# A two-layer encoder trunk on one core: weights of the up and down products laid out with two or four tiles of columns interleaved

## The chip, the cores and the metric

The kernel runs on one core of a Trainium2 chip. The metric is the device time of one execution in microseconds; lower is better. TensorE (PE) multiplies: it first loads a stationary operand of up to 128 x 128 (the instruction LDWEIGHTS, in the profile on a row of its own, PEld) and then streams a moving operand of up to 512 columns past it (MATMUL). VectorE (DVE), ScalarE (ACT) and GpSimd (POOL) do the rest; SyncE (SP) issues most transfers.

## What is computed

The reference takes x (512 tokens of width 1024) through two layers, in float32:

```
for i in range(DEPTH):                                   # DEPTH = 2
    h = rms_norm(x, attn_norm[i])
    mix = diff_attention(...) if i == 0 else gla_attention(...)
    cross = memory_cross_attention(...)
    x = x + concatenate([mix, cross]) @ w_out[i]
    h = rms_norm(x, ffn_norm[i])
    x = x + conv_ffn(h, w_up[i], conv_w[i], conv_b[i], w_down[i])

def conv_ffn(h, w_up, conv_w, conv_b, w_down):
    u = h @ w_up                       # 1024 -> 2 * 2816
    c = causal depthwise conv of width 3 over tokens (u) + conv_b
    a, g = split(c, 2)
    return (silu(g) * a) @ w_down      # 2816 -> 1024
```

The change lies in the two products of conv_ffn.

## The kernel before, in words

Activations lie transposed, features on the 128 partitions and the 512 tokens along the free dimension. For accuracy each float32 operand is split into a high part (rounded to the reduced float32 that TensorE takes at one pass) and a low part, and each product is made of three matmuls: high x high, high x low, low x high.

Weights come from one packed array, wpack, which the host lays out block by block in the order of use (function kernel, L1346 to L1351). A block is 128 partitions x 1024 floats. load_raw (L235) brings a block into a tile raw by a transfer on SP's queue, split_weights (L226) makes whi on ScalarE (the cast, L227) and wlo on VectorE (the difference, L230). _pieces (L57) lists the pieces of weights in order, _blocks (L95) cuts them into blocks, make_piece (L271) loads and splits them, prefetch (L289) keeps up to five blocks ahead.

Two groups of products use these weights as the stationary operand:

- The up products. w_up has 2 x 22 tiles of 128 columns (tile i of the half that becomes a, and of the half that is gated). One piece ("u", layer, i, half) is a block of eight tiles, one for each of the eight k of the contraction, tile k at columns 128 k to 128 k + 127. product (L343) takes hi[:, blk(n)] and lo[:, blk(n)] of each part as stationary operand and streams 512 tokens (L348 to L350): 24 matmuls for each piece.
- The down products. The 22 tiles of the middle are taken in three groups of 3, 4 and 4 pairs (GROUPS, L31). For each group the function down (L1154) forms seven products of sums of half blocks (a scheme in the manner of Strassen, with names such as a11, s1, a12) for each of two halves of the output: 14 steps. The sums are made of whole raw tiles by sum_weights (L242), and make_sum (L257) splits them (L263, L265). A step runs over the pairs k and, for each, two tiles n of 128 output features: stationary hi[:, 256 k + 128 n : ... + 128] or lo of the same, moving 256 tokens, both moving operand and output taken in reversed order (L1173). That makes 3 x 2 x 3 = 18 matmuls a step in the first group and 24 in the other two.

_ffn (L47) sets the order: up tiles 0 to 6, down group 0, up tiles 7 to 14, down group 1, up tiles 15 to 21, down group 2. TensorE's order is written out by hand; the up stages let VectorE and ScalarE work on convolution and SiLU, the down stages on adding each step's output into x (add, L1176) and on the weights of the steps to come.

In between, other projections (gemm, L314) use the weights as the moving operand; they are not touched.

Of the kernel before, what the change touches and what calls it, by code (L numbers as in the profile page):

```python
# [41 lines left out]
PASS = ([[(c, (0, 1, 2)) for c in C4], [(c, (3, 6, 7, 4, 5)) for c in C4]],  # L42
        [[(c, (0, 1, 2, 6, 7)) for c in (0, 1, 2)] + [(3, (0, 1, 2))],
         [(c, (3, 4, 5)) for c in (0, 1, 2)] + [(3, (6, 7, 3, 4, 5))]])


def _ffn():  # L47
# [9 lines left out]
def _pieces():  # L57

    plan = []

    def piece(key, name, i, ks, *ranges):
        plan.append((key, name, i, ks, ranges))

    for l in range(2):
        if l == 0:
            w = "w_in_diff"
            piece(("qk", 0), w, 0, K8, (0, 256), (768, 1024))
            piece(("vm", 0), w, 0, K8, (1536, 1792), (2304, 2560))
            piece(("qk", 1), w, 0, K8, (256, 512), (1024, 1280))
            piece(("kv", 0), "w_mem_kv", 0, K8, (0, 512))  # L70
            piece(("v", 1), w, 0, K8, (1792, 2304))
            piece(("qk", 2), w, 0, K8, (512, 768), (1280, 1536))
            piece(("kv", 1), "w_mem_kv", 1, K8, (0, 512))
        else:
            w = "w_in_gla"
            for i, ks in enumerate((GM[:3], GM[3:])):
                piece(("gm", i), w, 0, ks, (2304, 2576))
            for c in range(5):
                piece(("g", c), w, 0, K8, (512 * c, min(512 * c + 512, 2304)))
        for i, part in enumerate(PASS[l]):  # L80
            for c, ks in part:
                piece(("o", l, i, c), "w_out", l, ks, (256 * c, 256 * c + 256))
        base = 0
        for what, i in _ffn():
            if what == "up":
                for h in range(2):
                    f = DFF * h + 128 * i
                    piece(("u", l, i, h), "w_up", l, K8, (f, f + 128))
            else:
                for c, name in DOWN:  # L90
                    piece(("d", l, i, c, name), "w_down", l, (), (512 * c, 512 * c + 512))
    return plan


def _blocks():  # L95

    out = []
    for key, name, i, ks, ranges in _pieces():
        w = sum(b - a for a, b in ranges)
        if key[0] == "d":  # L100
            base, (f, _) = sum(GROUPS[:key[2]]), ranges[0]
            ks = [tuple(2 * q + j for q in range(base, base + GROUPS[key[2]])) for j in range(2)]
            out.append([(name, i, ks[j], ((f + 256 * h, f + 256 * h + 256),), 256)
                        for h, j in ((0, 0), (1, 0), (1, 1), (0, 1))] if key[4] == "a11" else [])
            continue
        step = WTILE // w
        out.append([(name, i, ks[j:j + step], ranges, w) for j in range(0, len(ks), step)])
    return out


# [40 lines left out]
def trunk(ctx, tc, head_d, x_t, mem_t, wpack, cols_a_d, cols_d, conv_d, gate_d, rel_bias, diff_lambda, consts, onehot, out):  # L151
# [31 lines left out]
    def blk(b, w=128):  # L183
        return slice(w * b, w * b + w)
# [36 lines left out]


    plan, blocks, made = _pieces(), _blocks(), []
    at = [0]

    def split_weights(c, raw, hi, lo, pin=False):  # L226
        ins = A.copy(hi[:, c], raw[:, c])  # L227
        if pin:
            tc.keep_in_program_order(ins)
        V.tensor_sub(lo[:, c], raw[:, c], hi[:, c].bitcast(F32))  # L230

    def raw_tile():
        return wp.tile([128, WTILE], F32, name="raw", tag="raw", bufs=RAWS)

    def load_raw(raw, n):  # L235
        nc.sync.dma_start(raw[:, :n], wpack[at[0], :, :n])
        at[0] += 1
        return raw
# [32 lines left out]
    def make_piece(raws=None, between=None):  # L271
        key = plan[len(made)][0]
        if key[0] == "d":
            made.append(make_sum(key))
            return
        parts = []
        for i, (_, _, kk, _, w) in enumerate(blocks[len(made)]):
            n = len(kk)
            raw = load_raw(raw_tile(), n * w) if raws is None else raws[i]
            hi, lo = (wp.tile([128, WTILE], F32R, name=t, tag=t, bufs=WB) for t in ("whi", "wlo"))  # L280
            if between is not None and i == 3:
                between()
            split_weights(slice(0, n * w), raw, hi, lo, len(made) == 2)
            parts += [(hi[:, blk(j, w)], lo[:, blk(j, w)]) for j in range(n)]
        made.append(parts)

    used = [0]
# [147 lines left out]
    with tc.tile_pool(name="ini", bufs=1) as ip, tc.manual_schedule(engines={E.Activation, E.DVE, E.Pool, E.SP}):  # L435
# [7 lines left out]
        p = bank("tp")  # L443
# [24 lines left out]
        parts, acc, split_w = [], [None], [None]  # L468
# [20 lines left out]
        for k in range(KT):  # L489
# [12 lines left out]
            hi, lo = parts[k]  # L502
            terms = (xh[k], hi), (xh[k], lo), (xl[k], hi)
            todo = [(b, i) for b in range(NB) for i in range(3)]
            for b, i in sorted(todo, key=lambda bi: bi[1]) if k == 0 else todo:
                xp, w = terms[i]
# [599 lines left out]
    def ffn(pool, l, acc):  # L1106
# [47 lines left out]
        def down(g, mids, finish):  # L1154
            last, ks = len(mids) - 1, tuple(range(len(mids)))
            parts, banks, first, last_group = {}, {}, used[0], g + 1 == len(GROUPS)

            def step(c, tag, w, m, ks=ks, start=False, more=True):
                if (c, w) not in parts:
                    parts[c, w] = weights(("d", l, g, c, w), more)  # L1160
                elif more:
                    prefetch(first + more)
                if start:
                    banks[c, tag] = bank(tag)
                p = banks[c, tag]
                hi, lo = parts[c, w]
                for k in ks:
                    mh, ml = mids[k][m]
                    for n in range(2):
                        o, ws = p[:, blk(n, 256)], slice(256 * k + 128 * n, 256 * k + 128 * n + 128)  # L1170
                        terms = (hi, mh), (hi, ml), (lo, mh)
                        for i, (a, b) in enumerate(terms):
                            mm(o[:, ::-1], a[:, ws], b[:, ::-1], start=start and (k, n, i) == (0, 0, 0), stop=k == last and i == 2,  # L1173
                               skip_group_check=True)

            def add(c, tag, f, t):  # L1176
                x = xpair[2 * c + f][:, :, blk(t, 256)]
                V.tensor_add(x, x, banks[c, tag].rearrange("p (n s) -> p n s", n=2))  # L1178

            def done(c, f, t=None):  # L1180
                for n in range(2):
                    finish(4 * c + 2 * f + n, t)
            if not last_group:
                step(0, "lg", "a11", "b11", start=True)
                add(0, "lg", 0, 0)
                step(0, "tp", "s1", "t1", start=True)
                add(0, "tp", 1, 1)
                step(0, "mm", "a12", "b21", start=True)
                add(0, "mm", 0, 0)
            else:  # L1190
                step(0, "lg", "a11", "b11", ks[:-1], True)
                step(0, "tp", "s1", "t1", ks[:-1], True, False)
                step(0, "mm", "a12", "b21", ks[:-1], True, False)
                step(0, "lg", "a11", "b11", ks[-1:], more=False)
                add(0, "lg", 0, 0)
                step(0, "tp", "s1", "t1", ks[-1:], more=1)
                add(0, "tp", 1, 1)
                step(0, "mm", "a12", "b21", ks[-1:], more=2)
                add(0, "mm", 0, 0)
            step(0, "lg", "s2", "t2")  # L1200
            add(0, "lg", 0, 1)
            step(0, "tp", "s4", "b22")
            add(0, "tp", 0, 1)
            step(0, "lg", "s3", "t3")
            add(0, "lg", 1, 1)
            step(1, "lg", "a11", "b11", start=True)
            add(1, "lg", 0, 0)
            step(0, "lg", "a22", "t4")
            add(0, "lg", 1, 0)
            done(0, 0)  # L1210
            step(1, "tp", "s1", "t1", start=True)
            add(1, "tp", 1, 1)
            step(1, "lg", "s2", "t2")
            add(1, "lg", 0, 1)
            done(0, 1)
            if l == 0 and last_group:
                tables("natural_log_exp_and_others")
            step(1, "mm", "a12", "b21", start=True)
            add(1, "mm", 0, 0)
            done(1, 0, 0)  # L1220
            step(1, "lg", "s3", "t3")
            add(1, "lg", 1, 1)
            done(1, 1, 1)
            step(1, "tp", "s4", "b22")
            add(1, "tp", 0, 1)
            done(1, 0, 1)
            step(1, "lg", "a22", "t4")
            add(1, "lg", 1, 0)
            done(1, 1, 0)
# [38 lines left out]
        for what, i in _ffn():  # L1268
            if what == "up":
# [12 lines left out]
                if i % 2 == 0:  # L1282
                    w = pool.tile([128, 8, 256], F32, name="w", bufs=1)
# [3 lines left out]
            else:  # L1287
                n, last = GROUPS[i], i == len(GROUPS) - 1
# [93 lines left out]
```

## Time and profile before

| what | us |
|---|---|
| median of the runs shown (2 runs, 1168.51 to 1169.13) | 1168.82 |
| the profiled execution, its own time | 1169.78 |
| its span, from the first to the last instruction | 1167.9 |
| third up stage of layer 0 (up tiles 15 to 21), stretch 490.1 to 566.2 | 76.1 |
| second down group of layer 0, stretch 450.3 to 490.1 | 39.8 |
| third down group of layer 0, stretch 566.2 to 607.8 | 41.6 |

Columns of a profile's views: a timeline row is start in us, length in us, engine, line of the kernel, operation, tiles (out<-in), partitions x elements, count. In the chain of work that ended last, a row is start, length, what. A group row has count, busy us, mean ns of one, and the idle time before. Matmuls overlap each other in the records, since one is still draining while the next streams: the pace is the distance from one start to the next, not the length of one. The same holds for the loads.

### The profile page before, as it was taken

How to read it: one execution, taken by the hardware profiler on the slowest of the kernel's cores; microseconds unless marked ns; L12 is line 12 of the kernel's file. 1: busy time of each engine (PE TensorE's matmuls, PEld its weight loads, DVE VectorE, ACT ScalarE, POOL GpSimd, SP SyncE). 2: the span in 40 equal slices, each digit the busy share in tenths (PEclk: the TensorE clock that was granted, in tenths of full speed). 3: DMA queues.
4: the chain of work that ended last, by engine and by line, in shares of the span. 5: the costliest groups of instructions: out<-in, count | busy, mean ns of one | idle time of the engine just before them, and what ended most of it. 6: DMA issues, size and time to landing. Idle time of an engine off the chain costs nothing.

```text
span 1167.9 us, 16705 instructions
## 1 busy us (share of the span) xinstructions
PE 1153.8 (99%) x6448; PEld 986.4 (84%) x6448; DVE 886.4 (76%) x1454; ACT 598.9 (51%) x1048; POOL 4.1 (0%) x17
## 2 busy tenths in 40 slices
PE   9999999999999999999999999999999999999998
PEld 6877777788899889988898788988789988998888
DVE  7746677679986778668897746868998777876885
ACT  6847677556443444344467534436654344434441
POOL 0000000000000000000000000000000000000000
PEclk9999999999999999999999999999999999999999
DMA  8533213233126322522253221144222532253212
GB/s 289 176 99 99 68 55 125 61 112 105 63 67 195 91 73 72 163 91 72 66 157 124 73 73 46 47 161 126 86 68 64 183 105 74 73 150 103 72 37 73
DMA packets 39853, 117.94 MB, mean 101 GB/s; under 512 B 4735, under 2 KB 7608, under 8 KB 39774
## 3 DMA queue, kind: packets, MB, share of 16 engines
q1 hardware_dynamic: 39630, 116.62, 32.1%
q8 instruction: 51, 0.84, 0.3%
q10 hardware_dynamic: 144, 0.26, 0.1%
q14 instruction: 28, 0.23, 0.1%
HBM read 112.65 MB, written 4.21 MB: 100 GB/s over the span
## 4 chain that ended last, share of the span: by engine, by line
PE 86%; DVE 8%; ACT 2%; DMA 1%; issue 1%; SPq 0%; DVEq 0%; ACTq 0%
PE ps_mm L348 9%; PE ps_mm L349 9%; PE ps_mm L350 9%; PE ps_lg L1173 8%; PE ps_sm L348 7%; PE ps_sm L350 7%; PE ps_sm L349 7%; PE ps_mm L327 5%; PE ps_mm L329 5%; PE ps_mm L328 5%; PE ps_tp L1173 4%; PE ps_mm L1173 2%; PE ps_tp L196 2%; DVE wlo L265 1%; PE ps_lg L686 1%; PE ps_sm L722 1%
## 5 line engine op out<-in xcount | busy, mean ns | idle before, releaser
L230 DVE TENSOR_TENSOR wlo<-raw,whi 128x1024 fp32r<-128x1024 f32 (+4 forms) x164 | 186.5, 1140 | 86.4 <-ACT whi L227 85.4
L227 ACT CAST whi<-raw 128x1024 fp32r<-128x1024 f32 (+4 forms) x164 | 160.7, 986 | 154.2 <-PE ps_sm L349 69.7
L348 PE MATMUL ps_mm<-x,whi 128*128 128x512 f32 x438 | 172.6, 394 | 0.3 <-DVE midh L1264 0.3
L349 PE MATMUL ps_mm<-x,whi 128*128 128x512 f32 x438 | 170.6, 389 | 0.2 <-DVE x L309 0.2
L350 PE MATMUL ps_mm<-x,wlo 128*128 128x512 f32 x438 | 170.6, 390 | 0.0
L348 PE MATMUL ps_sm<-x,whi 128*128 128x512 f32 x378 | 148.0, 391 | 0.0
L350 PE MATMUL ps_sm<-x,wlo 128*128 128x512 f32 x378 | 147.1, 389 | 0.0
L349 PE MATMUL ps_sm<-x,whi 128*128 128x512 f32 x378 | 147.1, 389 | 0.0
L327 PE MATMUL ps_mm<-whi,x 128*128 128x512 f32 (+2 forms) x336 | 132.0, 393 | 0.0
L329 PE MATMUL ps_mm<-whi,x 128*128 128x512 f32 (+2 forms) x336 | 126.7, 377 | 0.5 <-DVE x L309 0.4
L328 PE MATMUL ps_mm<-wlo,x 128*128 128x512 f32 (+2 forms) x336 | 126.0, 375 | 0.0
L263 ACT CAST whi<-raw 128x1024 fp32r<-128x1024 f32 (+1 forms) x60 | 58.4, 979 | 85.6 <-PE ps_sm L349 26.2
L348 PEld LDWEIGHTS ps_mm<-x,whi 128*128 128x128 f32 x438 | 82.3, 188 | 17.3 <-issue 0.9
L350 PEld LDWEIGHTS ps_mm<-x,wlo 128*128 128x128 f32 x438 | 82.2, 188 | 17.3
L349 PEld LDWEIGHTS ps_mm<-x,whi 128*128 128x128 f32 x438 | 82.3, 188 | 16.9 <-DVE x L309 0.6
L265 DVE TENSOR_TENSOR wlo<-raw,whi 128x1024 fp32r<-128x1024 f32 (+1 forms) x60 | 67.9, 1131 | 24.8 <-ACT whi L263 24.8
L349 PEld LDWEIGHTS ps_sm<-x,whi 128*128 128x128 f32 x378 | 71.0, 188 | 14.9 <-issue 0.5
L348 PEld LDWEIGHTS ps_sm<-x,whi 128*128 128x128 f32 x378 | 71.0, 188 | 14.9 <-issue 0.5
L350 PEld LDWEIGHTS ps_sm<-x,wlo 128*128 128x128 f32 x378 | 71.0, 188 | 14.9
L1173 PE MATMUL ps_lg<-midh,whi 128*128 128x256 f32 x264 | 74.8, 283 | 2.4 <-DVE x L1178 2.4
L1173 PE MATMUL ps_lg<-midh,wlo 128*128 128x256 f32 x264 | 74.3, 282 | 0.0
L1173 PE MATMUL ps_lg<-midl,whi 128*128 128x256 f32 x264 | 74.3, 282 | 0.0
(308 smaller groups left out, 2279.6 us busy)
## 6 DMA issues: line engine op xcount, KB each, us to landing
raw<-in_wpack_dram SPq DMA_DIRECT2D x170, 512.0 KB, 3.6
raw<-in_wpack_dram SPq DMA_DIRECT2D x24, 384.0 KB, 3.1
x<-in_x_t_dram SPq DMA_DIRECT2D x15, 256.0 KB, 5.4
xres<-x SPq DMA_DIRECT2D x8, 256.0 KB, 3.7
x<-xres SPq DMA_DIRECT2D x8, 256.0 KB, 4.6
raw<-in_wpack_dram SPq DMA_DIRECT2D x7, 256.0 KB, 6.7
bt<-bias_d SPq DMA_DIRECT2D x6, 256.0 KB, 5.1
x<-in_mem_t_dram SPq DMA_DIRECT2D x4, 256.0 KB, 6.0
```

Source lines behind the costliest of these rows:

```text
L196: nc.tensor.transpose(dst, src, ident[:n, :n])
L227: ins = A.copy(hi[:, c], raw[:, c])
L230: V.tensor_sub(lo[:, c], raw[:, c], hi[:, c].bitcast(F32))
L263: A.copy(hi[:, c], raw[:, c])
L265: todo = [lambda: V.tensor_sub(lo[:, c], raw[:, c], hi[:, c].bitcast(F32)), lambda: [sum_weights((*key[:3], *x)) for x in after]]
L327: mm(p, sh[k][:, blk(b)], hi, start=k == 0, stop=False)
L328: mm(p, sh[k][:, blk(b)], lo, start=False, stop=False)
L329: mm(p, sl[k][:, blk(b)], hi, start=False, stop=k == KT - 1)
L348: mm(p, hi[:, blk(n)], bh, start=i == first, stop=False)
L349: mm(p, hi[:, blk(n)], bl, start=False, stop=False)
L350: mm(p, lo[:, blk(n)], bh, start=False, stop=i == last)
L1173: mm(o[:, ::-1], a[:, ws], b[:, ::-1], start=start and (k, n, i) == (0, 0, 0), stop=k == last and i == 2, skip_group_check=True)
```

## The change

Within a block, tiles of 128 columns are interleaved in twos or fours: at step s, column c of tile j stands at 128 (j - j mod s) + s c + (j mod s), where it stood at 128 j + c. The stationary operand of tile j is then read with a step of s floats: 8 bytes at s = 2, 16 bytes at s = 4. A new function _step gives s: for up pieces 1 below tile 8, 2 for tiles 8 to 14, 4 for tiles 15 to 21; for down pieces 1, 2 and 4 in groups 0, 1 and 2; 1 for all others. The host packs accordingly, make_piece and down slice accordingly. Nothing else is changed: the same values, instructions, order, tiles and transfers.

```
+def _step(key):
+    if key[0] == "u":
+        return 1 if key[2] < 8 else 2 if key[2] < 15 else 4
+    if key[0] == "d":
+        return (1, 2, 4)[key[2]]
+    return 1
...
 def _blocks():
...
-        out.append([(name, i, ks[j:j + step], ranges, w) for j in range(0, len(ks), step)])
+        out.append([(name, i, ks[j:j + step], ranges, w, _step(key)) for j in range(0, len(ks), step)])
...
         def make_piece
-            parts += [(hi[:, blk(j, w)], lo[:, blk(j, w)]) for j in range(n)]
+            at_ = [slice(w * (j - j % step) + j % step, w * (j - j % step) + step * w, step) for j in range(n)]
+            parts += [(hi[:, c], lo[:, c]) for c in at_]
...
         down, step
-                        o, ws = p[:, blk(n, 256)], slice(256 * k + 128 * n, 256 * k + 128 * n + 128)
+                        s = _step(("d", l, g))
+                        j = 2 * k + n
+                        o, ws = p[:, blk(n, 256)], slice(128 * (j - j % s) + j % s, 128 * (j - j % s) + 128 * s, s)
...
         kernel (host)
-        wpack[i, :, :len(ks) * w] = t.transpose(1, 0, 2).reshape(128, -1)
+        t = t.transpose(1, 0, 2)
+        if step > 1:
+            t = t.reshape(128, -1, step, 128).transpose(0, 1, 3, 2)
+        wpack[i, :, :len(ks) * w] = t.reshape(128, -1)
```

More of the change, by code (lines that the diff above doesn't have):

```diff
@@ L102, in _blocks @@
             ks = [tuple(2 * q + j for q in range(base, base + GROUPS[key[2]])) for j in range(2)]
-            out.append([(name, i, ks[j], ((f + 256 * h, f + 256 * h + 256),), 256)
+            out.append([(name, i, ks[j], ((f + 256 * h, f + 256 * h + 256),), 256, _step(key))
                         for h, j in ((0, 0), (1, 0), (1, 1), (0, 1))] if key[4] == "a11" else [])
@@ L276, in make_piece @@
         parts = []
-        for i, (_, _, kk, _, w) in enumerate(blocks[len(made)]):
+        for i, (_, _, kk, _, w, step) in enumerate(blocks[len(made)]):
             n = len(kk)
@@ L1347 @@
     wpack = np.zeros((len(blocks), 128, WTILE), np.float32)
-    for i, (name, l, ks, ranges, w) in enumerate(blocks):
+    for i, (name, l, ks, ranges, w, step) in enumerate(blocks):
         t = f[name][l].reshape(-1, 128, f[name].shape[-1])[list(ks)]
         t = np.concatenate([t[:, :, a:b] for a, b in ranges], axis=-1)
-        wpack[i, :, :len(ks) * w] = t.transpose(1, 0, 2).reshape(128, -1)
+        t = t.transpose(1, 0, 2)
+        if step > 1:
+            t = t.reshape(128, -1, step, 128).transpose(0, 1, 3, 2)
+        wpack[i, :, :len(ks) * w] = t.reshape(128, -1)
     go = f["gla_out_norm"][0]
```

## The prediction

> **What bounds the kernel now.** I read the page first (busy shares, slices, chain), then the windows of the stages that the change touches, then the chain and the timeline for the pace of single matmuls, and last the weight loads by form.
>
> The page:
>
> ```profile
> span 1167.9 us, 16705 instructions
> PE 1153.8 (99%) x6448; PEld 986.4 (84%) x6448; DVE 886.4 (76%) x1454; ACT 598.9 (51%) x1048; POOL 4.1 (0%) x17
> PEclk9999999999999999999999999999999999999999
> PE 86%; DVE 8%; ACT 2%; DMA 1%; issue 1%; SPq 0%; DVEq 0%; ACTq 0%
> ```
>
> TensorE is busy for 1153.8 of 1167.9 us at a steady clock, and the chain that ended last is TensorE work for 86%. A change of the pace of a matmul therefore goes into the time almost undiluted; what VectorE and ScalarE do is cover.
>
> The windows of the up and down stages that the change touches, first layer 0, then layer 1. Columns: stretch, length, then busy time and instruction count of PE and of PEld (weight loads), then the other engines:
>
> ```profile
> 363.30:450.30 87.00, 87.00 (x386) 72.05 (x385) 63.03 (x81) 38.01 (x50) 0.00 (x0) 1.00 0.29 90
> 450.30:490.10 39.80, 39.80 (x338) 39.77 (x337) 32.90 (x37) 16.46 (x17) 0.00 (x0) 1.00 0.43 133
> 490.10:566.20 76.10, 76.10 (x338) 63.04 (x337) 54.66 (x69) 32.63 (x42) 0.00 (x0) 1.00 0.28 83
> 566.20:607.80 41.60, 40.28 (x338) 39.89 (x338) 37.26 (x50) 24.03 (x35) 1.04 (x2) 1.00 0.39 116
> ...
> 1046.70:1122.90 76.20, 76.20 (x339) 63.12 (x338) 54.64 (x69) 32.70 (x43) 0.00 (x0) 1.00 0.27 83
> 1122.90:1164.00 41.10, 40.11 (x337) 39.72 (x335) 29.05 (x34) 12.80 (x14) 0.00 (x0) 1.00 0.18 59
> ```
>
> Read the PE and PEld columns against the length. In the up stages (363 to 450, 490 to 566) PE is busy throughout and the loads take 83% of the stretch. In the down stages (450 to 490, 566 to 608) the loads take 96 to 100% as well. So an up stage has some room for a longer load, and a down stage has none.
>
> The pace of one matmul. In the timeline of the third up stage, matmuls of 512 moving columns; 177 rows stand from the first to the last line below:
>
> ```profile
> 490.08 0.39 PE L348 MATMUL ps_sm<-x,whi 128*128 128x512 f32 x1
> ...
> 529.98 0.39 PE L350 MATMUL ps_mm<-x,wlo 128*128 128x512 f32 x1
> ```
>
> (529.98 - 490.08) / 176 = 226.7 ns from start to start. (The 0.39 us is one matmul from start to end; they overlap.) The chain in the second down stage, pieces of 24 matmuls of 256 reversed moving columns:
>
> ```profile
> 450.49 2.84 PE ps_lg L1173 x24
> ...
> 487.41 2.84 PE ps_lg L1173 x24
> ```
>
> 2.84 / 24 = 118.3 ns. The same size read forwards, in the last projection of the second layer; 26 rows from first to last:
>
> ```profile
> 750.95 0.28 PE L329 MATMUL ps_mm<-whi,x 128*128 128x256 f32 x1
> ...
> 753.95 0.28 PE L327 MATMUL ps_mm<-whi,x 128*128 128x256 f32 x1
> ```
>
> 3.00 / 25 = 120.0 ns. Forward against forward, 256 more columns cost 226.7 - 120.0 = 106.7 ns, that is 0.417 ns per column. What is left is a fixed part of 120.0 - 106.7 = 13.3 ns per matmul; in the reversed down products it is 118.3 - 106.7 = 11.6 ns.
>
> **The change part by part.** It adds and removes no instruction on any engine, no transfer and no wait. The packing on the host only permutes columns inside a block, so the transfers of raw, the ScalarE casts, the VectorE differences and the sums s1 to s4 run on whole tiles as before: cost nothing. What changes is the address pattern of the weight loads in four places of each layer. Counts from the windows and the code: up tiles 8 to 14 at step 2 are 7 tiles x 2 halves x 8 k x 3 terms = 336 loads per layer (of the 386 in the window; 48 more are tile 7, which stays at step 1), up tiles 15 to 21 at step 4 again 336 (window x338), the second down group at step 2 336, and the third at step 4 336. For two layers: 672 each of up step 2, up step 4, down step 2, down step 4, in all 2688 of the 6448 loads. The first down group and up tiles 0 to 7 are untouched.
>
> No load in this trace has a step other than 1, so its price has to be bounded. The loads by form:
>
> ```profile
> L1173 PEld LDWEIGHTS ps_lg<-midh,wlo 128*128 128x128 f32 x264 | 49.7, 188 | 0.0
> L196 PEld LDWEIGHTS ps_tp<-C,em 128*128 128x128 f32 x92 | 11.4, 141 | 2.8 <-issue 0.2
> L619 PEld LDWEIGHTS ps_tp<-em,vm 128*64 128x64 f32 x64 | 3.4, 136 | 1.6 <-ACT em L711 0.8 <-issue 0.5 <-ACT rs_y L217 0.3
> L196 PEld LDWEIGHTS ps_tp<-C,q 128*96 128x96 f32 x16 | 1.9, 126 | 0.2
> ```
>
> and eight loads of 128 columns in a row behind which nearly nothing streams (matmuls of one column):
>
> ```profile
> 615.18 0.97 PEld L422 LDWEIGHTS ps_sm<-C,xt 128*128 128x128 f32 x8 [0.35 <-DVE xt L1078]
> ```
>
> A load of 128 columns lasts 188 ns, one of 64 columns 136 ns: (188 - 136) / 64 = 0.81 ns per column, 104 ns for 128, the rest latency. Back to back they follow each other every (0.97 - 0.19) / 7 = 111 ns: 104 and about 7. In the transposes a column costs only (141 - 126) / 32 = 0.47 ns. So an operand's read delivers a word of four bytes per 0.42 ns at best (the moving columns) or 0.47 ns (the transposes' loads), and the loads of this change go at half of that pace, 0.81 ns.
>
> Lower end of the price: the fixed 13.3 or 11.6 ns per matmul could go altogether: 1344 up x 13.3 + 1344 down x 11.6 = 17.9 + 15.6 = 33.5 us gained. Upper end: the read has to pass the skipped words too, at the fastest pace shown. Step 2 then sweeps 256 words, 107 to 120 ns; step 4 512 words, 213 to 241 ns, to which the 7 ns come.
>
> I take the sweep at 0.417 ns a word, since the moving operand shows that pace on unbroken words of the same kind. Then, in turn:
>
> Up, step 2: a load takes 107 + 7 = 114 ns beside a matmul of 226.7 ns: hidden. 0 us. Down, step 2: 114 ns in a slot of 118.3 ns: hidden with 4 ns to spare. 0 us. Up, step 4: 213 + 7 = 220 ns in 226.7: just hidden, the thinnest cover in this sum; at 241 + 7 = 248 ns it would cost 21 x 672 = 14 us. Down, step 4: 220 ns in a slot of 118.3: the load becomes the bound, 672 x (220 - 118.3) = 68.3 us (at 248 ns 87 us).
>
> [...]
>
> A small term the other way. In the step-4 down stages TensorE waits for VectorE's adds into x:
>
> ```profile
> PE ps_lg L1173 <- DVE x L1178: 2.4, 4, 1.0
> ```
>
> Three of these four waits, 2.3 us, lie in the third down groups (the fourth, 0.2, in the first). With a step of 24 matmuls at 5.3 us instead of 2.8, VectorE's add comes in time: -2 us. Nothing else is late: VectorE is busy 37 of 41.6 us there and gets 34 us more; the transfers and casts only gain room.
>
> Sum, against the profiled execution's own 1169.78 us (span 1167.9 and 1.9 around it; 1.0 above the median of the runs shown, a tenth of a per cent): 1169.8 + 0 + 0 + 0 + 68.3 - 2 = 1236.
>
> **The rivals.**
>
> The load goes by its columns alone, and the change does nothing. If each column is fetched by an access of its own, 0.81 ns, whatever lies between, step 4 costs what step 1 costs: 1169.8, say 1165 to 1174. For it: the load's pace is half of what the read can deliver, so there may be slack for one line per column. Against: nothing in the trace shows how far that slack goes.
>
> Each new line of the load steals time from the moving stream. The fixed part might be such theft. For it: where the stream is slow the fixed part nearly goes:
>
> ```profile
> 704.93 0.81 PE L1000 MATMUL ps_sm<-gv,x 128*128 128x192 f32 x4
> ```
>
> and its line's durations (least, median, most):
>
> ```profile
> L1000 PE MATMUL ps_sm<-gv,x x32: 323/324/328, 704.9 to 777.1; 128*128 128x192 f32 x32
> ```
>
> Four of those matmuls start every (0.81 - 0.324) / 3 = 162 ns for 192 columns, 0.84 ns a column, twice the 0.417; at exactly twice, 160 ns, only 2 ns are fixed, though the loads are as long (188 ns). So the 13 ns look like two fast reads in each other's way. If the theft goes by the stretch swept, it doubles at step 2 and is fourfold at step 4: 672 x (13.3 + 11.6) + 672 x 3 x (13.3 + 11.6) = 16.7 + 50.2 = 66.9 us, time 1169.8 + 66.9 - 2 = 1235. Same sum, other places: every changed stage is longer, the up stages too. Against it: a read that steals per column would not care about the step. [...]
>
> Both at once: step 2 16.7 us, up step 4 672 x 39.9 = 26.8, down step 4 bound by the load, 68.3: 1169.8 + 111.8 - 2 = 1280.
>
> The other side: the theft is a collision of two sweeps, and the steps end it. Today the moving read passes words at 0.417 ns and the load at 0.81 ns, so one overtakes the other again and again; at step 2 both pass addresses at one speed and, once apart, stay apart. For it: reversing the moving read alone already moved the spacing from 120.0 to 118.3 ns, so the order of addresses does count. Against: that moved 1.7 ns of 13. If the fixed part vanishes at step 2 alone, 672 x (13.3 + 11.6) = 16.7 us are gained: 1153; if at step 4 too, 1136. It decides for faster by 2% (1145.4) only when three quarters of the fixed part go in all four places, and it is lost as soon as step 4 in the down stages costs 25 ns a load (672 x 25 = 16.8 us).
>
> **How the numbers follow.** The load as the bound in step-4 down stages, 1236: 0.32. Theft by stretch, 1235: 0.15. Both, 1280: 0.10. Nothing, 1170: 0.33. Fewer collisions, 1153 or 1136: 0.10. The first two give one time, together 0.47, so 1236 is predicted. Its own range is 1222 to 1262 (the upper end with the transposes' pace, 0.47 ns a word, in the down stages, 87 us, and part of the up stages' 14). The range has to reach down to the case of no effect and its fringe, and up to that end: 1160 to 1262 leaves out the two cases of 0.10. Slower by over 2% (over 1192): 0.32 + 0.15 + 0.10 = 0.57. Within 2%, about what a measurement of this kernel can tell from no change: 0.33, and 0.07 of the collisions' 0.10, 0.40. Faster: 0.03.
>
> **What would show it.** In the profile after: the third down group's chain pieces of 24 matmuls at 5.3 us (2.84 now), its window 65 to 75 us long instead of 41.6, PEld busy throughout, and the wait for x at L1178 gone from it; the second down group still at 2.84; the up tiles at 226.7 ns in all three parts. The recorded length of a step-4 load should grow from 188 to about 300 ns. Step-2 stages that get longer, or up stages at 240 to 267 ns, would show theft. If the third group stays at 2.84, the load does not pay for what it skips and the forecast is wrong; if any of the four goes below its pace of now, the collisions were the cause.

## The result and the profile after

The changed kernel takes 1253.66 us (median of 2 runs, 1253.39 to 1253.92) against 1168.82 before: 1.0726 times as long, 95% interval 1.068 to 1.0772. It is slower by 84.8 us.

The page of the changed kernel:

```profile
span 1251.5 us, 16705 instructions
PE 1240.7 (99%) x6448; PEld 1099.7 (88%) x6448; DVE 888.7 (71%) x1454; ACT 600.6 (48%) x1048; POOL 4.1 (0%) x17
PEclk9999999999999999999999999999999999999999
PE 92%; DVE 5%; ACT 2%; issue 1%; DMA 0%; ACTq 0%; DVEq 0%
```

The instructions are the same to the last one, the clock is the same, VectorE and ScalarE are busy for the same time (888.7 and 600.6 us against 886.4 and 598.9). TensorE alone is longer: 87 us more of matmuls, 113 us more of weight loads. (Lines of code have moved: 348 to 350 are now 358 to 360, 1173 is 1185.)

The windows of the same stages, columns as before:

```profile
362.40:451.70 89.30, 89.30 (x386) 73.88 (x385) 63.37 (x81) 38.07 (x50) 0.00 (x0) 1.00 0.28 88
451.70:492.00 40.30, 40.30 (x337) 40.29 (x336) 32.66 (x36) 16.52 (x17) 0.00 (x0) 1.00 0.43 132
492.00:571.10 79.10, 79.10 (x338) 79.10 (x337) 54.83 (x69) 32.77 (x43) 0.00 (x0) 1.00 0.27 80
571.10:649.30 78.20, 78.20 (x337) 78.20 (x337) 41.08 (x53) 25.32 (x35) 1.04 (x2) 1.00 0.25 82
...
1169.10:1247.60 78.50, 78.47 (x337) 78.27 (x336) 29.84 (x34) 13.21 (x14) 0.00 (x0) 1.00 0.09 31
```

In layer 0 the stage with up tiles at step 2 grew from 87.0 to 89.3 us, the second down group (step 2) from 39.8 to 40.3, the up tiles at step 4 from 76.1 to 79.1, and the third down group (step 4) from 41.6 to 78.2. The last alone costs 36.6 us in this layer and 37.4 in the other. Where PEld had gaps in the third up stage (63.0 us of 76.1), it has none now (79.1 of 79.1): the records of the step-4 loads leave no gap beside a 512-column matmul.

The pace from start to start. Chain pieces of 24 matmuls, the second and the third down group:

```profile
454.76 2.88 PE ps_tp L1185 x24
...
587.97 5.60 PE ps_lg L1185 x24
```

2.88 / 24 = 120.0 ns at step 2 (118.3 before) and 5.60 / 24 = 233.3 at step 4. Up tiles at step 2, 87 rows from first to last, then at step 4, again 87:

```profile
379.84 0.39 PE L359 MATMUL ps_mm<-x,whi 128*128 128x512 f32 x1
...
399.90 0.39 PE L358 MATMUL ps_mm<-x,whi 128*128 128x512 f32 x1
```

```profile
499.68 0.40 PE L360 MATMUL ps_sm<-x,wlo 128*128 128x512 f32 x1
...
519.89 0.39 PE L359 MATMUL ps_sm<-x,whi 128*128 128x512 f32 x1
```

20.06 / 86 = 233.3 ns and 20.21 / 86 = 235.0 ns, against 226.7. (Over a whole step-4 up stage, its slower start included, it is 79.1 us / 336 = 235.4 ns.) The loads themselves (least, median and most in ns), of an up and a down stage at step 4:

```profile
L358 PEld LDWEIGHTS ps_sm<-x,whi x59: 308/310/311, 494.7 to 569.5; 128*128 128x128 f32 x59
```

```profile
L1185 PEld LDWEIGHTS ps_lg<-midh,whi x42: 330/330/330, 587.7 to 644.4; 128*128 128x128 f32 x42
```

They had lasted 188 ns. At step 2 they last 193 and 198.

What is left of TensorE's waits for the adds into x, 2.4 us in four waits before:

```profile
PE ps_lg L1185 <- DVE x L1190: 0.2, 1, 0.2
```

It is the one in the first down group; the 2.3 us in the third groups are gone.

### The profile page after: what moved, and what is told of

The parts are those of the page before. It is cut to its first block, busy times and chain, and to the rows that moved or that the text cites. A ratio compares the mean times of both kernels' runs of the same rounds, so it can differ in the third digit from the quotient of the medians.

```text
span 1251.5 us, 16705 instructions
## 1 busy us (share of the span) xinstructions
PE 1240.7 (99%) x6448; PEld 1099.7 (88%) x6448; DVE 888.7 (71%) x1454; ACT 600.6 (48%) x1048; POOL 4.1 (0%) x17
## 4 chain that ended last, share of the span: by engine, by line
PE 92%; DVE 5%; ACT 2%; issue 1%; DMA 0%; ACTq 0%; DVEq 0%
PE ps_lg L1185 13%; PE ps_mm L358 8%; PE ps_mm L359 8%; PE ps_mm L360 8%; PE ps_sm L358 7%; PE ps_sm L360 7%; PE ps_sm L359 7%; PE ps_tp L1185 6%; PE ps_mm L337 5%; PE ps_mm L339 5%; PE ps_mm L338 5%; PE ps_mm L1185 3%; PE ps_tp L205 2%; PE ps_lg L696 1%; PE ps_sm L732 1%; PE ps_mm L517 1%
## 5 line engine op out<-in xcount | busy, mean ns | idle before, releaser
L358 PE MATMUL ps_sm<-x,whi 128*128 128x512 f32 x378 | 149.8, 396 | 0.0
L359 PE MATMUL ps_sm<-x,whi 128*128 128x512 f32 x378 | 148.7, 393 | 0.0
L358 PEld LDWEIGHTS ps_mm<-x,whi 128*128 128x128 f32 x438 | 94.6, 216 | 13.9 <-issue 0.9
L360 PEld LDWEIGHTS ps_mm<-x,wlo 128*128 128x128 f32 x438 | 94.6, 216 | 13.6
L359 PEld LDWEIGHTS ps_mm<-x,whi 128*128 128x128 f32 x438 | 94.7, 216 | 13.3 <-DVE x L319 0.6
L358 PEld LDWEIGHTS ps_sm<-x,whi 128*128 128x128 f32 x378 | 87.1, 230 | 10.2 <-issue 0.5
L359 PEld LDWEIGHTS ps_sm<-x,whi 128*128 128x128 f32 x378 | 87.1, 230 | 10.2 <-issue 0.5
L360 PEld LDWEIGHTS ps_sm<-x,wlo 128*128 128x128 f32 x378 | 87.0, 230 | 9.9
L1185 PE MATMUL ps_lg<-midh,whi 128*128 128x256 f32 x264 | 86.0, 326 | 0.2 <-DVE x L1190 0.2
L1185 PE MATMUL ps_lg<-midh,wlo 128*128 128x256 f32 x264 | 85.7, 325 | 0.0
L1185 PE MATMUL ps_lg<-midl,whi 128*128 128x256 f32 x264 | 85.7, 325 | 0.0
```

Source lines behind the costliest of these rows:

```text
L358: mm(p, hi[:, blk(n)], bh, start=i == first, stop=False)
L359: mm(p, hi[:, blk(n)], bl, start=False, stop=False)
L360: mm(p, lo[:, blk(n)], bh, start=False, stop=i == last)
```

## The experiments

Where no ratio is given, a kernel was run once, and what is read from it is the pace of many matmuls, not a small difference of the time.

**The parts alone.** Two kernels that change only the function _step: steps in the up tiles alone, and steps in the down groups alone.

```
up tiles alone:
     if key[0] == "u":
-        return 1 if key[2] < 8 else 2 if key[2] < 15 else 4
+        return (1, 2, 4)[0 if key[2] < 8 else 1 if key[2] < 15 else 2]
     if key[0] == "d":
-        return (1, 2, 4)[key[2]]
+        return (1, 1, 1)[key[2]]

down groups alone:
     if key[0] == "u":
-        return 1 if key[2] < 8 else 2 if key[2] < 15 else 4
+        return (1, 1, 1)[0 if key[2] < 8 else 1 if key[2] < 15 else 2]
     if key[0] == "d":
         return (1, 2, 4)[key[2]]
```

> Steps 1, 2, 4 in the up tiles as in the changed kernel, step 1 in all down groups. Theory (each place pays for itself): the up stages keep what they had in the changed kernel, 233.3 ns a matmul at step 2 and 235.4 at step 4 against 226.7: 672 x 6.7 + 672 x 8.7 = 10.3 us over the kernel before, 1179 us. Rival (the longer up stages are an after-effect of the down stages, whose weights and adds run into them): both up stages go back to 226.7 ns and the time to 1169 us.

Measured: 1179.73 us, ratio 1.0093 (1.0078 to 1.0108); 233.3 and 235.4 ns in the two up stages, 118.3 in both down groups.

> Step 1 in all up tiles, steps 1, 2, 4 in the down groups as in the changed kernel. Theory (the load at step 4 is the bound of the third down group): 120.0 ns a matmul at step 2, 233 at step 4, 672 x 1.7 + 672 x 114.7 = 78 us less the 2 to 4 us of waits that go: 1243 us. Rival (an after-effect of the up stages): below 1180 us.

Measured: 1243.11 us, ratio 1.0634 (1.0616 to 1.0652); 120.0 and 233.0 ns in the down groups, 226.7 in the up stages. Over the kernel before, run beside them at 1168.9 us, the two parts cost 10.8 and 74.2 us, 85.0 together, where the whole costs 84.8. Each place pays for itself; both rivals fall.

**Other steps.** Down groups at 3, 8 and 4, up tiles 8 to 14 at 8:

```
-        return 1 if key[2] < 8 else 2 if key[2] < 15 else 4
+        return (1, 8, 4)[0 if key[2] < 8 else 1 if key[2] < 15 else 2]
...
-        return (1, 2, 4)[key[2]]
+        return (3, 8, 4)[key[2]]
```

> Other steps: down groups 3, 8 and 4, up tiles 1 (0 to 7), 8 (8 to 14) and 4 (15 to 21). Sweep theory (the load passes every word it skips, which is how the forecast was made): with the 233 ns of step 4 made of 7 ns and 226 for 512 words, step 3 gives 7 + 170 = 177 ns, step 8 gives 7 + 452 = 459 ns, in the down and in the up stage alike; in all some 1660 us. Line theory (a load pays once for each stretch of 16 bytes that it touches, and nothing for stretches that it jumps over): step 8 costs what step 4 costs, 233 ns in the down and 235 in the up stage, step 3 touches three stretches for four words, 7 + 170 = 177 ns as well; in all some 1360 us. [...]

Measured: 1374 us. Chain pieces: 18 matmuls of the first group (step 3), then 24 of the second (step 8) and of the third (step 4):

```profile
338.57 3.21 PE ps_mm L1185 x18
...
476.00 5.87 PE ps_tp L1185 x24
...
648.12 5.60 PE ps_lg L1185 x24
```

178 ns at step 3, 245 at step 8, 233 at step 4; the up tiles at step 8 run at 245 as well. The sweep, on which the forecast was made, wants 459 at step 8 and falls. A step twice as long, over stretches that hold no wanted word, costs 5% more, not 100%. From step 2 on, what counts in the main is how many stretches of 16 bytes, called lines here and in the prediction's rivals, the 128 words lie in: 64 at step 2 (120 ns), 96 at step 3 (178), 128 at step 4 (233) and at step 8 (245). The size is worked out from these four paces: of stretches of 8 bytes there would be 128 at step 2 already, as at step 4, and of 32 bytes 64 at step 4 and 128 at step 8. From 96 to 128 it is (233.0 - 178.3) / 32 = 1.71 ns a line. The line theory isn't exact either: it had 233 ns for step 8 and some 1360 us, and the 10 to 12 ns by which a matmul at step 8 is longer than that, at as many lines, stay open; over 1344 matmuls they make the 14 us between 1360 and 1374. The columns alone, on which the prediction's first rival rests, don't set the price: the same 128 columns make a slot of 178 ns at step 3 and of 245 at step 8.

**The moving operand at step 2.** If a line has a price, the other read should pay it too. All stationary operands at step 1, and in the second down group the moving ones are read out of two neighbouring blocks:

```
-                op.update((t, (hi[:, i], lo[:, i])) for i, t in enumerate(names))
+                fh, fl = (t[:, 0:2].rearrange("p a b -> p (a b)") for t in (hi, lo))
+                op.update((t, (fh[:, i % 2:512:2], fl[:, i % 2:512:2])) for i, t in enumerate(names))
```

> Step 1 for all stationary operands; in the second down group the moving operand (256 columns) is read with a step of two words out of two neighbouring blocks, so that group multiplies other numbers and the output is another. Theory (each line of 16 bytes costs any read 1.67 to 1.8 ns, which is what the moving read needs for its four words at step 1: 4 x 0.417): 128 lines, 213 to 233 ns and some 12 fixed, 220 to 245 ns a matmul in the second down group, some 70 us more in all, 1240. [...]

Measured: 1247 us. The chain and the loads of the second down group:

```profile
456.05 5.60 PE ps_tp L1189 x24
```

```profile
L1189 PEld LDWEIGHTS ps_lg<-midh,whi x45: 208/208/209, 466.8 to 525.6; 128*128 128x128 f32 x45
```

233.3 ns a matmul, the same number as for the loads at step 4, while the loads here are the short ones. 256 words at step 2 lie in 128 lines, 128 words at step 4 too. This read doesn't keep its pace with two words of a line, 233.3 ns where step 1 has 118.3: at step 1 it takes a word every 0.417 ns and so spends 1.67 ns on each line, and at step 2 a line still takes about that (233.3 / 128 = 1.82 ns, the fixed part included) though only half of its words are wanted. The loads take a word every 0.81 ns; at step 2 the two words of a line take 1.62 ns, about what a line costs, which would explain why step 2 is nearly free for them (120.0 ns a matmul against 118.3). One thing this run doesn't exclude: step 2 alone was tried on the moving operand, so a read that halves its pace at any step would look the same. The lines of 16 bytes are worked out from the paces of the loads at steps 2, 3, 4 and 8; for the moving operand the price fits, and no more.

**The loads with little beside them.** Most down matmuls cut to 64 columns, steps 1, 2 and 4 as in the changed kernel:

```
+NARROW = 64
...
-                            mm(o[:, ::-1], a[:, ws], b[:, ::-1], ...
+                            m_ = slice(None, None, -1) if k == 0 and i == 0 else slice(NARROW - 1, None, -1)
+                            mm(o[:, m_], a[:, ws], b[:, m_], ...
```

> The changed kernel, but of the 24 (18) matmuls of a down step only the first of each half streams 256 columns, all others 64; three quarters of the products are left out, so the output is another. It shows the pace of the loads by themselves at steps 1, 2 and 4 in the three down groups. Theory (a step-4 load is the bound by its own length, the stream adds little): 111 to 113 ns at step 1, 111 to 120 at step 2, 220 to 233 at step 4. Rival (the load is slow only because the stream beside it reads from the same memory): at step 4 well below 200 ns once the stream is a quarter as long.

Measured: 1355 us, and the clock was halved for most of these stages, which nobody had expected. In the first 4 to 6 us of each it was still full, and there the question can be answered. Matmuls of the second group (step 2), 36 starts from the first line to the second, then of the third (step 4), 12 starts:

```profile
473.18 0.28 PE L1187 MATMUL ps_lg<-x,wlo 128*128 128x64 f32 x1
...
477.43 0.28 PE L1187 MATMUL ps_tp<-x,wlo 128*128 128x64 f32 x1
```

```profile
621.23 0.40 PE L1187 MATMUL ps_lg<-x,wlo 128*128 128x64 f32 x1
...
624.03 0.40 PE L1187 MATMUL ps_lg<-x,wlo 128*128 128x64 f32 x1
```

At full clock that is 4.25 / 36 = 118.1 ns at step 2 and 2.80 / 12 = 233.3 at step 4; in the first group (step 1) it is 112.0, and the second layer gives the same. All three come out as the theory had them. At step 4 the pace is that of the full stream, though the stream is a quarter as long: the 233 ns are the load's own, and the rival falls. The rest of the stages, with a stretch at full clock between (the clock is the number behind POOL's):

```profile
480.00:538.00 58.00, 58.00 (x274) 58.00 (x273) 27.00 (x28) 12.13 (x12) 0.00 (x0) 0.50 0.26 80
620.50:624.50 4.00, 4.00 (x19) 4.00 (x19) 2.64 (x3) 1.88 (x3) 0.00 (x0) 1.00 0.21 49
625.00:695.00 70.00, 70.00 (x301) 70.00 (x301) 37.94 (x50) 22.99 (x32) 1.04 (x2) 0.50 0.23 72
```

At half the clock the loads at steps 1 and 2 took 213 ns, nearly twice the 112 and 118 of full clock, while 70 us still hold 300 starts at step 4 (the count has one that reaches in): 233 ns. So the step-4 pace didn't follow the granted clock: 233 ns at 1.00 and at 0.50.

**Directions.** The 6.7 ns that up matmuls lose at step 2 are no load that is too long (193 ns in a slot of 233), so they ask for another reason. One kernel with the changed steps and all directions turned round, and one with step 1 and some turned:

```
+    def turned(t, rev):
+        return t[:, ::-1] if rev else t
...
+            o, bh, bl = (turned(t, rev) for t in (p, bh, bl))        # product, the up tiles
...
-                            mm(o[:, ::-1], a[:, ws], b[:, ::-1], ...
+                            mm(turned(o, _turn(("d", l, g))), a[:, ws], turned(b, _turn(("d", l, g))), ...
```

> The changed kernel's steps, with the direction of the moving operand and of the output turned round: the up products read reversed, the down products forwards. Theory (the load's own length is the bound at step 4, and at step 2 the load's additional lines disturb the stream whatever the direction): up 233 ns at step 2 and 235 at step 4, down 233 at step 4, each within 2 ns; down at step 2 within 2 ns of 120. Rival (two sweeps collide, and it is the relative direction that makes the loss): at step 2, where both sweep at one speed, turning one changes the pace by more than 4 ns, up below 229 or down above 124.

Measured: 1257 us; up 233.3 at step 2 and 233.7 at step 4, down 120.0 and 233.0. At step 2 the direction makes nothing, and the collision rival falls there. But up tiles 0 to 7, at step 1 and now reversed, ran at 233.3 as well.

> Step 1 everywhere as in the kernel before; the moving operand and the output are read reversed in up tiles 0 to 14 and in down groups 0 and 2, forwards in up tiles 15 to 21 and in down group 1. Theory (reversal saves 1.7 ns of a matmul's fixed part, as between 120.0 and 118.3 ns at 256 columns): up tiles 0 to 14 at 225.0 ns instead of 226.7, down group 1 at 120.0: 1440 x 1.7 - 672 x 1.7 = 1.3 us faster than the kernel before, 1167.5. Rival (the longer matmuls have room enough to absorb it and stay at 226.7): 1 us slower, 1170.

Measured: 1179.32 us, ratio 1.0093 (1.0076 to 1.011). Both expectations missed. Up tiles at step 1, moving operand and output reversed, 87 rows:

```profile
379.79 0.40 PE L370 MATMUL ps_mm<-x,whi 128*128 128x512 f32 x1
...
399.86 0.40 PE L369 MATMUL ps_mm<-x,whi 128*128 128x512 f32 x1
```

20.07 / 86 = 233.4 ns: reversing makes a matmul of 512 columns 6.7 ns slower, though it makes one of 256 columns 1.7 ns faster (the second down group, forwards here, ran at 120.0). 1440 x 6.7 + 672 x 1.7 = 10.8 us explain the loss of 10.5. The moving read and the output were always turned together, so which of the two costs the 6.7 ns isn't told.

**Half as many columns.** Up matmuls of 512 cut into two of 256, steps 1, 2 and 4 in the up tiles:

```
+                for t in (blk(0, 256), blk(1, 256)):
+                    mm(p[:, t], a[:, blk(n)], b[:, t], ...
```

> Down groups at step 1, up tiles at steps 1, 2 and 4; in up tiles 2 to 21 each matmul of 512 tokens is cut into two of 256, so each weight load is done twice, all read forwards. It asks whether the 6.7 ns that an up matmul of 512 columns loses at step 2 belong to the load. Theory (every step-2 load takes those 6.7 ns from the stream beside it, by its doubled lines): tiles 2 to 7 120.0 ns a matmul, tiles 8 to 14 126.7, tiles 15 to 21 233. Rival (the loss belongs to the matmul of 512 columns, not to the load; in the run with turned directions 256 forward columns ran at 120.0 at step 1 and at 120.0 at step 2): tiles 8 to 14 at 120.0 to 121, tiles 15 to 21 at 233. Time about 1340 us by both.

Measured: 1347 us; windows inside tiles 8 to 14 and tiles 15 to 21:

```profile
388.00:448.00 60.00, 60.00 (x502) 60.00 (x501) 41.22 (x53) 25.76 (x34) 0.00 (x0) 1.00 0.24 80
510.00:570.00 60.00, 60.00 (x259) 60.00 (x258) 21.23 (x27) 13.23 (x18) 0.00 (x0) 1.00 0.16 53
```

60 us hold 500 starts (the count has one or two that reach in from before): 120.0 ns at step 2, as at step 1, and 233.3 at step 4. The loss at step 2 is bound to the 512 columns; that every step-2 load takes 6.7 ns from the stream beside it is refuted.

**One load in three.** In the up tiles the low parts alone at step 2 (tiles 8 to 14), the high parts alone (tiles 15 to 21), written so by the splits:

```
+SPLIT = ((1, 1), (1, 2), (2, 1))
...
+                A.copy(view(hi, sh), view(raw, 1))
+                V.tensor_sub(view(lo, sl), view(raw, 1), view(hi, sh).bitcast(F32))
```

> Step 1 in the packing and in all down groups; in the up tiles the low part alone is written and read at step 2 in tiles 8 to 14 (one load in three), the high part alone in tiles 15 to 21 (two loads in three). It asks whether the 6.7 ns of an up matmul at step 2 belong to the matmul that a step-2 load runs beside. Theory (they do): one start in three 233.3 and two 226.7 ns apart in tiles 8 to 14, mean 228.9; two in three in tiles 15 to 21, mean 231.1; 672 x 2.2 + 672 x 4.4 = 4.5 us, 1173 us. Rival (the loss is a state that the whole sequence of matmuls falls into): one pace for all three, 226.7 or 233.3. ScalarE's and VectorE's splits write with a step here; should they get so long that TensorE waits for weights, the time says nothing and the paces between waits do.

Measured: 1177 us, where the theory had 1173. Tiles 8 to 14:

```profile
386.20 0.39 PE L367 MATMUL ps_sm<-x,whi 128*128 128x512 f32 x1
...
389.66 0.39 PE L367 MATMUL ps_sm<-x,whi 128*128 128x512 f32 x1
```

15 starts on, (389.66 - 386.20) / 15 = 230.7 ns (231.1 over the whole stage), with 230.0 to 232.5 for each of the three terms; tiles 15 to 21 run at 233.3. One load in three brings two thirds of the loss, two in three bring all of it, and it spreads over the neighbours. Neither theory fits: it isn't each load's own, and it isn't one state or none.

**Step 2 everywhere.**

```
     if key[0] == "u":
-        return 1 if key[2] < 8 else 2 if key[2] < 15 else 4
+        return (2, 2, 2)[0 if key[2] < 8 else 1 if key[2] < 15 else 2]
     if key[0] == "d":
-        return (1, 2, 4)[key[2]]
+        return (2, 2, 2)[key[2]]
```

> Step 2 in all up tiles and all down groups. Theory (the paces found add up place by place): 2112 up matmuls x 6.7 ns + 1848 down matmuls x 1.7 ns = 14.2 + 3.1 us over the kernel before: 1186 us. Rival (step 2 hurts only beside step 4, where the stages differ in layout): 1169 us.

Measured: 1185.00 us, ratio 1.0139 (1.0122 to 1.0156); 233.3 ns in all up tiles, 120.0 in all down groups. The paces add up to within 1 us. No kernel tried here beats the one before: step 1, forwards at 512 columns and reversed at 256, has the best pace of each kind.

## Why the prediction was right, and where it was off

The time lay in the range and on the side forecast, and the path in the sum is the one that came: the step-4 loads become the bound of the third down group, step 2 is nearly free, the waits for VectorE's adds there vanish (2.3 us, forecast as 2). It wasn't the likeliest single case: it had 0.32, no effect 0.33, and the range reached down to no effect, so that the time fell into it says little. The paces say more. 84.8 us came where 66 were forecast; term by term, against the paces measured:

- Down, step 4: 220 ns forecast, 233.0 measured: 672 x (233.0 - 118.3) = 77.1 us instead of 68.3. This is the largest error. The forecast was 213 ns for the sweep and 7 for what parts two loads. The loads with little beside them take 118.1, 178.3 and 233.3 ns for 64, 96 and 128 lines (the 178.3 beside 256 columns), 1.8 to 1.9 ns a line if all of it is put on the lines; how much of the 233 is a fixed part isn't settled. The third groups' windows, 78.2 and 78.5 us, are longer than the 65 to 75 forecast for the same reason.
- Up, step 4: called just hidden, 0 us. The slot grew from 226.7 to 235.4, 672 x 8.7 = 5.8 us. With a load that needs 233 ns by itself, the thin cover of 6.7 ns was gone.
- Up, step 2: 0 us forecast, 672 x 6.7 = 4.5 measured. The load was hidden as forecast, since by itself it takes 118.1 ns; the loss has another cause, which stays open.
- Down, step 2: 0 forecast, 672 x 1.7 = 1.1 measured. The 120.0 ns are also what 256 columns read forwards take at step 1: what is lost is the gain of reversing. That a down stage has no room for a longer load was read a shade too strictly: the loads' records overlap, so a busy PEld doesn't show it, and by themselves the step-1 loads take 112.0 ns of the slot of 118.3.

These make 88.5 us, less 2.3 for the waits 86.2; the measured 84.8 is 1.4 us below that, which isn't traced further.

The reason given was wrong in kind, and that it gave nearly the right price is luck. The forecast let the read pass every skipped word at 0.417 ns; the runs show that what it pays for is in the main, at steps 2 to 8, each line of 16 bytes that it touches (1.8 to 1.9 ns a line). At step 4 the two can't be told apart, since each line then holds one wanted word: 512 words at 0.417 ns are 213 ns, and so are 128 lines at the 1.67 ns that the moving read spends on one. At step 8 they part: the sweep asks for 459 ns there, the lines for 233, and 245 came.

The rivals. That the change does nothing is refuted by the result. Theft from the stream in proportion to the stretch swept, which would have cost up matmuls 40 ns at step 4, is refuted: they lose 8.7, and 256 forward columns lose nothing at step 2. The step-2 stages did get longer, which the prediction named as a sign of theft, but by 6.7 and 1.7 ns a matmul instead of 13.3 and 11.6. That equal sweeps end collisions and gain time is refuted: nothing got faster.

What stays open is the 6.7 ns of a 512-column matmul. They come at step 2, and at step 1 when the moving operand and the output are reversed, and not twice when both; they don't come at 256 columns, and one load in three brings two thirds of them. Loads and matmuls overlap in the records (PE busy for 99% of the changed kernel's span, PEld for 88%), but which of the two reads' orders costs what couldn't be told by these runs.

## What to carry to other kernels

Count the lines of 16 bytes that a TensorE operand touches, not its words: here 64 lines made a slot of 118 to 120 ns, 96 lines of a load 178, 128 lines 227 to 245, with the lines of 64 and 128 in either of the two reads. The loads at step 1 stand outside this: their 32 lines took 112.0 ns. In this kernel a stationary operand of float32 could be read at a step of two words for 2 to 7 ns a matmul and not so at three or four (178 and 233 ns beside 256 columns, against 118); a moving one not even at two (233). And a load was hidden only by its own slot: beside 512 columns a step of four cost 9 ns, beside 256 columns 115.

## What the hardware showed unasked

A stage with matmuls of 64 columns and back-to-back loads fell to a granted clock of 0.50 within 4 to 6 us, in all six such stages, with PE and PEld busy throughout (58.00 of 58.00 us in the stretch shown); the up stages behind them had it back within 3 to 6 us. And the step-4 load didn't notice: 233 ns at either clock, where a step-1 load went from 112 to 213.

Turning the moving operand and the output backwards is not one thing: 1.7 ns faster at 256 columns (118.3 against 120.0), 6.7 ns slower at 512 (233.3 against 226.7).
